# The first product of the down projection, its weight loads and its stores, in a one-core encoder layer in f32

## The chip, the cores and the metric

The kernel runs on one core of one Trainium2 chip. Times are microseconds of device time for one execution of the whole program; where several runs were made, the median is given. The core has a matrix engine (TensorE, PE), three engines for element-wise work (VectorE, DVE; ScalarE, ACT; GpSimd, POOL), a fifth engine that issues DMAs (SyncE, SP), and 16 DMA engines that move data between the chip's memory and the on-chip buffer. Each engine runs its own instructions in order; engines wait for one another by semaphores. ACT can issue DMAs too; those stand in its own order of instructions.

## The reference

One layer of an encoder: two attention branches merged by gates, and then a squared-ReLU MLP with a residual sum, and a final normalisation. The case touches only the MLP:

```python
h = _rmsnorm(x, g_mlp)
x = x + jnp.square(jax.nn.relu(h @ w_up)) @ w_down      # w_up 1024 x 4096, w_down 4096 x 1024
...
return _rmsnorm(x, g_final)
```

It is applied to 1024 sample tokens and to 256 prompt tokens with the same weights, 1280 rows in all, everything in float32.

## The kernel before

The attention half, up to about 950 us, is the same in both kernels. The MLP comes in two stages.

Each float32 product is made of three passes of TensorE over operands split in a rounded part (`hi`) and a remainder (`lo`): `lo` with `hi`, `hi` with `lo`, `hi` with `hi`. Splitting is done by ACT (the copy that rounds, `whi`, `dhi`, `uhi`) and then DVE (the subtraction that leaves the remainder, `wlo`, `dlo`, `ulo`). Both matrix products use a Strassen-like scheme: seven block products in place of eight, with sums and differences of blocks made beforehand. The names A11, A12, A22, S1 to S4 are those of the seven left operands.

*Up stage.* The function `up(j, ...)` runs for j = 0 to 15. Each pass makes the seven products for 256 columns of the hidden layer (PE tiles `x`, `y`, `z`, `pv`, `sc`), applies the squared ReLU (`relu2` on ACT, `relu2_sum` on DVE, into tiles `u`), makes four of the seven left operands of the down projection by sums on POOL, and stores all seven to a scratch array `scr_u` in memory with seven DMAs on SP. The weights of the next pass are split meanwhile. At fixed points of a pass a generator, `hooks`, is moved one step; in the last pass this is `Down.begin`, which prepares the start of the down projection.

*Down stage.* `Down.go` works through the list `JOBS` of 28 pairs (n, g): n is one of the seven products, g one of four groups of the hidden layer. Groups are taken in two pairs, and within a pair the order is n = 0 to 6, each for both groups. A job is 60 matmuls (PE tile `dn`): five tiles of rows, four blocks of the hidden layer, three passes. Its left operand is fetched from `scr_u` (`fetch`, three DMAs into `uraw`) two jobs ahead and split one job ahead (`left`: `uhi`, `ulo`, and for the prompt rows `up`). Its right operand is a block of `w_down` (`block`, two DMAs of 512 KB into `raw`) or a difference of blocks made by POOL (`combine`, tile `t`), split by `right` into `dhi` and `dlo`. `ORDER` gives the left operand of each n: S1, A11, S2, S3, S4, A22, A12. `TO` gives the blocks of the result, C11 to C22, to which product n is added; the sum is taken by DVE on tiles `v`, which begin as the residual, loaded from scratch `scr_x` by `residual` with five DMAs.

Around the change the order is written out by hand: instructions run on each engine in the order in which the code issues them. So a DMA on SP waits behind the DMAs ahead of it, and so does everything behind a DMA on ACT. A DMA takes one of eight completion semaphores in turn, and is held until the eighth DMA before it has landed. In `begin` the first two blocks of `w_down`, (0,0,0) and (0,0,1), are loaded by ACT's queue, and the first job is n = 0, whose right operand is a difference that POOL makes of these two.

Of the kernel before, what the change touches and what calls it, by code (L numbers as in the profile page):

```python
# [10 lines left out]
F32 = mybir.dt.float32  # L11
# [24 lines left out]
TH = T // 2  # L36

A11, A12, S2, S3, S1, A22, S4 = range(7)
# [59 lines left out]
def encoder_kernel(  # L98
# [5 lines left out]
    nc = tc.nc  # L104
# [13 lines left out]
    w_down4 = w_down[0].rearrange("(g k p) n -> p g k n", p=P, k=2)  # L118
# [37 lines left out]
    class Wide:  # L156
# [9 lines left out]
        def block(self, b):  # L166
            name, k, dt, make = self.spec
            n = BLOCKS[b][1]
            per = min(k, (self.most if b == 2 else 4096) // 4 // n)
            for i in range(k // per):  # L170
                self.t[b, i] = make(f"{name}_{b}_{i}", (P, per, n), dt)
# [461 lines left out]
    def entering():  # L633

        nonlocal unit0
        fetch()
        yield
        yield
        unit0 = load_unit(0), load_bias(0, wslot)
        yield  # L640
        prepare()
        yield
# [26 lines left out]
    with ExitStack() as pre:  # L669
        late = pre.enter_context(tc.tile_pool(name="values", bufs=1))  # L670
# [237 lines left out]
    if True:  # L908
# [4 lines left out]
        def stage(name, shape=(P, 512), dt=F32, n=1):  # L913
            pool = both if name in ("c", "z") else now[0]
            return pool.tile(list(shape), dt, name=name, tag=name, bufs=n)
# [739 lines left out]
    C11, C12, C21, C22 = range(4)  # L1655

    TO = ((C22, C12), (C11,), (C12,), (C21, C22), (C12,), (C21,), (C11,))
    JOBS = [(n, 2 * p + i) for p in range(NG // 2) for n in range(7) for i in range(2)]

    class Down:  # L1660
        def __init__(self):
# [3 lines left out]
        def make(self, name, shape=(P, 2, 512), dt=F32):  # L1665
            return self.late.tile(list(shape), dt, name=name, tag="l4", bufs=8)

        def block(self, g, k, h, make=wslot, queue=None):

            b = self.blocks[g, k, h] = [make("raw", (P, 2, 512)) for _ in range(2)]  # L1670
            for i in range(2):
                j = 4 * g + 2 * i
                (queue or nc.sync).dma_start(b[i], w_down4[:, j : j + 2, k, 512 * h : 512 * h + 512])

        def loads(self, n, g):
            if n == 1:
                self.block(g, 1, 1, slot)
            elif n == 4:
                self.block(g, 1, 0, slot)
            elif n == 5 and g < NG - 2:  # L1680
                self.block(g + 2, 0, 0)
                self.block(g + 2, 0, 1)

        def combine(self, n, g):

# [67 lines left out]

        def begin(self):

            self.block(0, 0, 0, wslot, nc.scalar)
            self.block(0, 0, 1, slot, nc.scalar)
            self.fetch(*JOBS[0])
            yield
            self.combine(*JOBS[0])  # L1760
            yield
            yield
            self.block(1, 0, 0)
            self.block(1, 0, 1)
            yield
            self.right(*JOBS[0], slot)
            self.combine(*JOBS[1])
            yield
            self.left(*JOBS[0], 0)
            self.left(*JOBS[0], 1)  # L1770
            yield
            self.fetch(*JOBS[1])
            yield
            self.left(*JOBS[0], 2)

        def ahead(self, s):

            n, g = JOBS[s]
            one, two = (JOBS[i] if i < len(JOBS) else None for i in (s + 1, s + 2))
            if two:  # L1780
                self.fetch(*two)
            self.loads(n, g)
            if s in (0, 2, 4):
                self.residual((C22, C11, C21)[s // 2])
            if s == 0:
                self.residual(C12)
            if one:
                self.right(*one, slot if s == 0 else self.make)
            if two:
                self.combine(*two)  # L1790
            yield
            for k in range(3):
                if one:
                    self.left(*one, k)
                yield
# [67 lines left out]
    with ExitStack() as pre:  # L1863
# [21 lines left out]
            yield x, y, c1  # L1885

        begun = {}

        def up(j, b, parts, hooks):

            def prompt_out(ps, dst):
                for i, d in enumerate(dst):
                    relu2(d[:, 512:], ps[:, P * i : P * i + P])

            u = [stage(f"u{i}", TH) for i in range(7)]
            u11, u12, u22, u21 = u[A11], u[A12], u[A22], u[S3]
            start = begin(parts)
            if j not in begun:  # L1900
                next(start)
            z = bank("sc", "z")
            nb = np_ = None
            steps_of(b, 2)
            next(hooks, None)
            x, y, c1 = begun[j] if j in begun else next(start)
            relu2_sum(u11[:, :512], y, c1)
            steps_of(b, 2)
            if j:
                pa = prompt(parts[0])  # L1910
            if j + 1 < FF // P // 2:
                np_ = []
                nb = right_up(j + 1, np_)
                next(nb)
            next(hooks, None)
            seven(x, S2, parts[1], 0, False, False)
            c2 = stage("c2", 512)
            nc.scalar.activation(c2, x, AF.Copy)
            if j:
                prompt_out(pa, (u11, u21))  # L1920
            steps_of(b, 2)
            next(hooks, None)
            seven(z, S3, parts[1], 1, last=False)
            c7 = stage("c7", 512)
            nc.scalar.activation(c7, z, AF.Copy)
            if not j:
                steps_of(nb, 2)
            next(hooks, None)
            seven(x, S1, parts[2], 0, False, False)
            relu2_sum(u22[:, :512], x, c7)  # L1930
            next(hooks, None)
            if nb and j:
                steps_of(nb, 3)
            seven(z, A22, parts[2], 1, False)
            relu2_sum(u21[:, :512], z, c2)
            next(hooks, None)
            if not j:
                *_, begun[1] = begin(np_)
            seven(x, S4, parts[3], 1, False)
            relu2(u12[:, :512], x)  # L1940
            next(hooks, None)
            if not j:
                steps_of(nb, 4)
                prompt_out(prompt(parts[0]), (u11, u21))
            prompt_out(prompt(parts[3], "sc"), (u12, u22))
            nc.gpsimd.tensor_tensor(u[S1], u21, u22, op=ALU.add)  # L1946
            nc.gpsimd.tensor_tensor(u[S2], u[S1], u11, op=ALU.subtract)
            nc.gpsimd.tensor_tensor(u[S3], u11, u21, op=ALU.subtract)
            nc.gpsimd.tensor_tensor(u[S4], u12, u[S2], op=ALU.subtract)
            for i in (A11, S1, A22, S2, S3, A12, S4):  # L1950
                nc.sync.dma_start(scr_u[j // 4][:, i, j % 4, :], u[i])
            next(hooks, None)
            return nb, np_

# [16 lines left out]
        down = Down()  # L1971
        last = FF // P // 2 - 1
        for j in range(last + 1):
            b = up(j, *b, entering() if not j else down.begin() if j == last else iter(()))

    down.go()

# [23 lines left out]
```

## Time and profile before

| what | before |
|---|---|
| median of three runs | 1692.16 us |
| the three runs | 1690.64, 1692.16, 1692.21 us |
| profiled execution, its own time | 1693.05 us |
| profiled execution, span | 1691.3 us |
| mean granted TensorE clock | 0.997 |
| PE busy | 1670.7 us (99%) |
| DVE, ACT, POOL busy | 950.1, 721.3, 514.9 us |

The span runs from the first to the last instruction of the profiled execution; its own time is 1.75 us more. In rows of the timeline the columns are the start, the time, the engine, the line, the operation with its output and inputs, and the shape; in square brackets stands how long the engine idled before it and what ended the idling. ACTq and SPq are the DMA issues on ACT and SP. In rows of waits the three numbers are the sum, the count and the longest. In rows of windows each engine has its busy time and, in parentheses, its number of instructions; behind them stand PEclk, the granted TensorE clock as a share of full speed, the mean share of the DMA engines in use, and the rate in GB/s.

### The profile page before, as it was taken

How to read it: one execution, taken by the hardware profiler on the slowest of the kernel's cores; microseconds unless marked ns; L12 is line 12 of the kernel's file. 1: busy time of each engine (PE TensorE's matmuls, PEld its weight loads, DVE VectorE, ACT ScalarE, POOL GpSimd, SP SyncE). 2: the span in 40 equal slices, each digit the busy share in tenths (PEclk: the TensorE clock that was granted, in tenths of full speed). 3: DMA queues.
4: the chain of work that ended last, by engine and by line, in shares of the span. 5: the costliest groups of instructions: out<-in, count | busy, mean ns of one | idle time of the engine just before them, and what ended most of it. 6: DMA issues, size and time to landing. Idle time of an engine off the chain costs nothing.

```text
span 1691.3 us, 24932 instructions
## 1 busy us (share of the span) xinstructions
PE 1670.7 (99%) x9268; PEld 1414.9 (84%) x9268; DVE 950.1 (56%) x1548; ACT 721.3 (43%) x1489; POOL 514.9 (30%) x404
## 2 busy tenths in 40 slices
PE   8999999999999999999999999999999999999998
PEld 7898888887788888888888888888887888888886
DVE  6733233455563565667378445455457767667575
ACT  6332323356562656654176333333334333333345
POOL 1312212212112472200100556455556322314150
PEclk9999999999999999999999999999999999999999
DMA  7416562567666893845121443343346744633333
GB/s 246 151 57 125 134 136 75 162 192 200 182 196 193 219 245 100 289 136 189 41 85 58 159 159 118 121 159 130 116 152 250 280 152 157 209 106 116 119 119 124
DMA packets 224408, 260.35 MB, mean 154 GB/s; under 512 B 29568, under 2 KB 154288, under 8 KB 224288
## 3 DMA queue, kind: packets, MB, share of 16 engines
q1 hardware_dynamic: 214976, 235.60, 43.9%
q0 software_dynamic: 7936, 20.54, 5.6%
q10 hardware_dynamic: 1376, 2.62, 0.4%
q8 instruction: 73, 1.20, 0.3%
q14 instruction: 47, 0.39, 0.1%
HBM read 173.03 MB, written 90.92 MB: 156 GB/s over the span
## 4 chain that ended last, share of the span: by engine, by line
PE 90%; DVE 4%; ACT 2%; DMA 2%; issue 1%; POOL 1%; SPq 0%; DVEq 0%; ACTq 0%; POOLq 0%
PE dn L347 20%; PE x L347 18%; PE mm L192 14%; PE z L347 9%; PE v L794 6%; PE mm L347 5%; PE y L347 5%; PE sc L347 2%; PE pv L347 2%; PE sc L537 1%; PE pv L1170 1%; PE pv L582 1%; PE pt L569 1%; PE pt L1155 1%; PE sc L1131 1%
## 5 line engine op out<-in xcount | busy, mean ns | idle before, releaser
L347 PE MATMUL dn<-dhi,ulo 128*128 128x512 f32 x448 | 175.7, 392 | 4.3 <-DVE ulo L186 4.3
L347 PE MATMUL dn<-dlo,uhi 128*128 128x512 f32 x448 | 175.2, 391 | 0.0
L347 PE MATMUL dn<-dhi,uhi 128*128 128x512 f32 x448 | 175.1, 391 | 0.0
L347 PE MATMUL x<-chi,wlo 128*128 128x512 f32 x424 | 167.3, 395 | 1.7 <-DVE wlo L314 1.6
L347 PE MATMUL x<-clo,whi 128*128 128x512 f32 x424 | 165.7, 391 | 0.1
L347 PE MATMUL x<-chi,whi 128*128 128x512 f32 x424 | 165.1, 389 | 0.0
L314 DVE TENSOR_TENSOR wlo<-ta,whi 128x1024 fp32r<-128x1024 f32 x30 | 55.7, 1857 | 179.1 <-ACT whi L312 179.1
L314 DVE TENSOR_TENSOR wlo<-raw,whi 128x1024 fp32r<-128x1024 f32 x60 | 92.5, 1541 | 96.7 <-ACT whi L312 96.7
L389 POOL TENSOR_TENSOR tb<-raw 128x512 f32<-128x512 f32 x25 | 32.7, 1308 | 364.4 <-DMA raw<-in_w_in_dram 147.8
L347 PEld LDWEIGHTS dn<-dhi,ulo 128*128 128x128 f32 x448 | 84.6, 189 | 23.2 <-DVE ulo L186 5.7
L186 DVE TENSOR_TENSOR ulo<-uraw,uhi 128x1024 fp32r<-128x1024 f32 x56 | 94.3, 1702 | 12.4 <-ACT uhi L185 12.4
L347 PEld LDWEIGHTS dn<-dhi,uhi 128*128 128x128 f32 x448 | 84.7, 189 | 17.8
L347 PEld LDWEIGHTS dn<-dlo,uhi 128*128 128x128 f32 x448 | 84.7, 189 | 17.4
L347 PEld LDWEIGHTS x<-chi,wlo 128*128 128x128 f32 x424 | 79.8, 188 | 18.1 <-DVE wlo L314 1.3
L347 PEld LDWEIGHTS x<-chi,whi 128*128 128x128 f32 x424 | 79.6, 188 | 17.0
L1699 POOL TENSOR_TENSOR t<-raw,t 128x1024 f32<-128x1024 f32 x16 | 47.7, 3001 | 147.0 <-DMA raw<-in_w_down_dram 147.0
L347 PEld LDWEIGHTS x<-clo,whi 128*128 128x128 f32 x424 | 79.8, 188 | 14.8 <-DVE clo L314 0.4
L1853 DVE TENSOR_TENSOR v<-v,dn 128x512 f32<-128x512 f32 x90 | 59.6, 681 | 40.4 <-PE dn L347 37.9
L1946 POOL TENSOR_TENSOR u<-u,u 128x640 f32<-128x640 f32 x16 | 26.1, 1630 | 160.0 <-ACT u L1871 160.0
L347 PE MATMUL dn<-dhi,up 128*128 128x512 f32 x224 | 73.5, 389 | 0.0
L347 PE MATMUL z<-chi,wlo 128*128 128x512 f32 x184 | 72.0, 391 | 0.0
L272 ACT ACTIVATE pt<-pt 128x512 f32<-128x512 f32 (+1 forms) x70 | 37.9, 543 | 79.5 <-PE pt L1155 45.0
(325 smaller groups left out, 4660.9 us busy)
## 6 DMA issues: line engine op xcount, KB each, us to landing
scr_u<-u SPq DMA_DIRECT2D x112, 320.0 KB, 2.6
uraw<-scr_u SPq DMA_DIRECT2D x56, 512.0 KB, 4.5
raw<-in_w_in_dram SPq DMA_DIRECT2D x33, 512.0 KB, 5.4
raw<-in_w_up_dram SPq DMA_DIRECT2D x32, 512.0 KB, 5.2
raw<-in_w_down_dram SPq DMA_DIRECT2D x28, 512.0 KB, 6.6
sg<-scr_g SPq DMA_DIRECT2D x32, 256.0 KB, 6.4
uraw<-scr_u SPq DMA_DIRECT2D x28, 256.0 KB, 4.7
v<-scr_v SPq DMA_DIRECT2D x96, 64.0 KB, 2.7
```

Source lines behind the costliest of these rows:

```text
L186: nc.vector.tensor_tensor(lo, src, hi.bitcast(F32), op=ALU.subtract)
L192: nc.tensor.matmul(ps, a, b, start=i == 0, stop=i == len(seq) - 1)
L272: nc.scalar.activation(out, in_, AF.Copy)
L314: nc.vector.tensor_tensor(lo, src, hi.bitcast(F32), op=ALU.subtract)
L347: nc.tensor.matmul(ps, a, b, start=first and i == 0, stop=last and i == len(seq) - 1, skip_group_check=True)
L389: (nc.vector if vector else nc.gpsimd).tensor_tensor(o, x, y, op=ALU.subtract)
L537: nc.tensor.matmul(at(k, h)[p0 : p0 + nq, :], qk[rows, p0 : p0 + nq], qk[rows, P + P * a : P + P * a + W], start=True, stop=True, skip_gro ...
L569: nc.tensor.transpose(ps[:, P * a : P * a + P], s[:, h, P * k : P * k + P], ident)
L794: nc.tensor.matmul(ps[:, :n], a, b, start=k == 0 and j == 0, stop=k == KC - 1 and j == 2)
L1699: nc.gpsimd.tensor_tensor(o, a, b, op=ALU.subtract)
L1853: nc.vector.tensor_tensor(v, v, ps, op=ALU.add)
L1946: nc.gpsimd.tensor_tensor(u[S1], u21, u22, op=ALU.add)
```

## The change

The first pair of groups now begins with n = 6, whose left operand is A12 and whose right operand is a plain block of `w_down`, (g,1,0), with no difference by POOL. The block for the first job is loaded in the pass before the last, into a buffer of the up stage; that for the second job in the last pass. All loads are issued by SP. The blocks (0,0,0) and (0,0,1) are loaded later in the last pass, (1,0,0) and (1,0,1) in the first job. The block (g,1,0) of the first pair is thus read twice, since the product n = 5 still needs it. The first blocks of the next pair are loaded with n = 4 in place of n = 5. The residual blocks are loaded one per job, C11 first. The seven stores of a pass are issued in the next pass behind its first products and its first hook. In the last pass the split of the right operand (`right`) stands at the third hook, ahead of the product S3, and the split of the left operand (`left`) follows the sum for `u22`.

```diff
-    JOBS = [(n, 2 * p + i) for p in range(NG // 2) for n in range(7) for i in range(2)]
+    JOBS = [(n, 2 * p + i) for p in range(NG // 2) for n in (range(7) if p else (6, *range(6))) for i in range(2)]
...
-        def block(self, g, k, h, make=wslot, queue=None):
+        def block(self, g, k, h, make=wslot):
...
-                (queue or nc.sync).dma_start(b[i], w_down4[:, j : j + 2, k, 512 * h : 512 * h + 512])
+                nc.sync.dma_start(b[i], w_down4[:, j : j + 2, k, 512 * h : 512 * h + 512])
 
         def loads(self, n, g):
-            if n == 1:
+            if n == 6 and g == 0:
+                self.block(1, 0, 0)
+                self.block(1, 0, 1)
+            elif n == 1:
                 self.block(g, 1, 1, slot)
             elif n == 4:
                 self.block(g, 1, 0, slot)
-            elif n == 5 and g < NG - 2:
-                self.block(g + 2, 0, 0)
-                self.block(g + 2, 0, 1)
+                if g < NG - 2:
+                    self.block(g + 2, 0, 0)
+                    self.block(g + 2, 0, 1)
...
         def begin(self):
 
-            self.block(0, 0, 0, wslot, nc.scalar)
-            self.block(0, 0, 1, slot, nc.scalar)
             self.fetch(*JOBS[0])
             yield
-            self.combine(*JOBS[0])
-            yield
-            yield
-            self.block(1, 0, 0)
-            self.block(1, 0, 1)
+            self.block(1, 1, 0)
             yield
             self.right(*JOBS[0], slot)
-            self.combine(*JOBS[1])
+            yield
+            self.fetch(*JOBS[1])
             yield
             self.left(*JOBS[0], 0)
             self.left(*JOBS[0], 1)
-            yield
-            self.fetch(*JOBS[1])
+            self.block(0, 0, 0)
+            self.block(0, 0, 1)
             yield
             self.left(*JOBS[0], 2)
...
-            if s in (0, 2, 4):
-                self.residual((C22, C11, C21)[s // 2])
-            if s == 0:
-                self.residual(C12)
+            if s < 4:
+                self.residual((C11, C22, C12, C21)[s])
...
+        stores_u = []
+
+        def store_u():
+            while stores_u:
+                nc.sync.dma_start(*stores_u.pop(0))
...
             next(hooks, None)
+            store_u()
+            u = [stage(f"u{i}", TH) for i in range(7)]
+            u11, u12, u22, u21 = u[A11], u[A12], u[A22], u[S3]
...
-            for i in (A11, S1, A22, S2, S3, A12, S4):
-                nc.sync.dma_start(scr_u[j // 4][:, i, j % 4, :], u[i])
+            stores_u.extend((scr_u[j // 4][:, i, j % 4, :], u[i]) for i in (A11, S1, A22, S2, S3, A12, S4))
...
+            if j == last - 1:
+                down.block(0, 1, 0, lambda name, shape: late.tile(list(shape), F32, name=name, tag="block", bufs=2))
             b = up(j, *b, entering() if not j else down.begin() if j == last else iter(()))
+        store_u()
```

The change moves instructions on the engines; three places show how. First SP, at the end of the last pass but one and in the last pass of the up stage. `scr_u_106` and `scr_u_107` are the groups 0 and 1 of the scratch array, `scr_u_109` group 3, which the last passes fill. Before:

```order
L1951 DMA scr_u_109<-u_12195 128x640
L1719 DMA uraw<-scr_u_106 128x2x512 x2
L1721 DMA uraw<-scr_u_106 128x4x128
L1673 DMA raw<-in_w_down_dram 128x2x512 x4
L1719 DMA uraw<-scr_u_107 128x2x512 x2
L1721 DMA uraw<-scr_u_107 128x4x128
L1951 DMA scr_u_109<-u_12392 128x640
```

And after the change:

```order
L377 DMA raw<-in_w_up_dram 128x8x128 x2
L1722 DMA uraw<-scr_u_106 128x2x512 x2
L1724 DMA uraw<-scr_u_106 128x4x128
L1888 DMA scr_u_109<-u_12214 128x640
L1888 DMA scr_u_109<-u_12218 128x640
L1888 DMA scr_u_109<-u_12219 128x640
L1888 DMA scr_u_109<-u_12216 128x640
L1888 DMA scr_u_109<-u_12217 128x640
L1888 DMA scr_u_109<-u_12215 128x640
L1888 DMA scr_u_109<-u_12220 128x640
L1673 DMA raw<-in_w_down_dram 128x2x512 x2
L1722 DMA uraw<-scr_u_107 128x2x512 x2
```

The seven stores of the last pass but one stood ahead of the first job's fetch and now stand behind it; two weight loads, those of the second job, stand behind the stores.

Second ACT, from the middle of the last pass to the start of the down projection (`c` are copies of a PE result, `u` the squared ReLU, `whi` the split of up weights, `dhi` and `uhi` that of a down job's right and left operand). Before:

```order
L1882 ACTIVATE c_12413<-x 128x512
L312 ACTIVATE whi<-ta 128x1024
L1673 DMA raw<-in_w_down_dram 128x2x512 x4
L312 ACTIVATE whi<-tb 128x1024
L1918 ACTIVATE c_12493<-x 128x512
L1870 ACTIVATE u_12392<-pv 128x128
L1871 ACTIVATE u_12392<-u_12392 128x128
L1870 ACTIVATE u_12395<-pv 128x128
L1871 ACTIVATE u_12395<-u_12395 128x128
L312 ACTIVATE whi<-raw 128x1024
L1925 ACTIVATE c_12515<-z 128x512
L185 ACTIVATE dhi<-t_12477 128x1024
```

And after:

```order
L312 ACTIVATE whi<-ta 128x1024
L312 ACTIVATE whi<-tb 128x1024
L1920 ACTIVATE c_12489<-x 128x512
L1866 ACTIVATE u_12423<-pv 128x128
L1867 ACTIVATE u_12423<-u_12423 128x128
L1866 ACTIVATE u_12426<-pv 128x128
L1867 ACTIVATE u_12426<-u_12426 128x128
L312 ACTIVATE whi<-raw 128x1024
L185 ACTIVATE dhi<-raw 128x1024 x2
L1927 ACTIVATE c_12519<-z 128x512
L185 ACTIVATE uhi<-uraw 128x1024 x2
L185 ACTIVATE up<-uraw 128x512
```

The four DMA issues between `whi<-ta` and `whi<-tb` are gone; both `dhi` now come from raw weights and stand ahead of the copy of `z`, and the two `uhi` directly behind it.

Third SP, as the down projection begins (`v` are the tiles of the result, `scr_x_96` to `scr_x_105` the rows of the residual). Before:

```order
L1951 DMA scr_u_109<-u_12398 128x640
L1719 DMA uraw<-scr_u_106 128x2x512 x2
L1721 DMA uraw<-scr_u_106 128x4x128
L1752 DMA v<-scr_x_100 128x512
L1752 DMA v<-scr_x_101 128x512
```

And after:

```order
L1888 DMA scr_u_109<-u_12429 128x640
L1722 DMA uraw<-scr_u_106 128x2x512 x2
L1724 DMA uraw<-scr_u_106 128x4x128
L1673 DMA raw<-in_w_down_dram 128x2x512 x4
L1755 DMA v<-scr_x_96 128x512
L1755 DMA v<-scr_x_97 128x512
L1755 DMA v<-scr_x_98 128x512
L1755 DMA v<-scr_x_99 128x512
L1755 DMA v<-scr_x_104 128x512
L1722 DMA uraw<-scr_u_107 128x2x512 x2
```

The last store and the third job's fetch stand as they did; four weight loads now stand between that fetch and the residual, of which C11 is the first block and five tiles are loaded in a job instead of ten.

More of the change, by code (lines that the diff above doesn't have):

```diff
@@ L1895, in prompt_out @@
                     relu2(d[:, 512:], ps[:, P * i : P * i + P])
-            u = [stage(f"u{i}", TH) for i in range(7)]
-            u11, u12, u22, u21 = u[A11], u[A12], u[A22], u[S3]
             start = begin(parts)
```

## The prediction

> **What bounds the kernel now.** I read first the busy time of each engine, then the waits of TensorE in the MLP half (950 us to the end).
>
> ```profile
> span 1691.3 us, 24932 instructions
> PE 1670.7 (99%) x9268; PEld 1414.9 (84%) x9268; DVE 950.1 (56%) x1548; ACT 721.3 (43%) x1489; POOL 514.9 (30%) x404
> PE dn L347 <- DVE ulo L186: 4.3, 3, 3.2
> ```
>
> TensorE (PE) is the bound. The change adds and removes no matmul, so only PE's waits and its pace can move the end. In the MLP half it waited three times, 4.3 us in all (longest 3.2), each time for a left-operand remainder `ulo`. The timeline of PE shows where:
>
> ```profile
> 1287.72 0.39 PE L347 MATMUL z<-chi,wlo 128*128 128x512 f32 x1
> ...
> 1296.09 0.28 PE L347 MATMUL sc<-phi,whi 128*128 128x256 f32 x1
> 1299.56 0.80 PE L347 MATMUL dn<-dhi,ulo 128*128 128x512 f32 x1 [3.19 <-DVE ulo L186]
> 1302.87 0.80 PE L347 MATMUL dn<-dhi,ulo 128*128 128x512 f32 x1 [0.38 <-DVE ulo L186]
> 1305.68 0.40 PE L347 MATMUL dn<-dlo,uhi 128*128 128x512 f32 x1
> ...
> 1316.34 0.39 PE L347 MATMUL dn<-dhi,ulo 128*128 128x512 f32 x1
> 1616.45 0.50 PE L347 MATMUL dn<-dhi,ulo 128*128 128x512 f32 x1 [0.75 <-DVE ulo L186]
> ```
>
> Two waits stand where the down projection begins: its first job starts at 1299.56, its second at 1316.34. The third, at 1616.45, is in a job that the change leaves in its place; I leave it as it is. The windows view (PE with its matmul count, then the other engines, PEclk, DMA share, GB/s) shows that the wait also cost pace:
>
> ```profile
> 1299.50:1305.60 6.10, 5.66 (x13) 4.02 (x14) 6.10 (x4) 2.13 (x3) 6.02 (x3) 0.53 0.11 40
> 1305.60:1310.00 4.40, 4.40 (x22) 3.60 (x21) 4.40 (x3) 0.00 (x0) 4.40 (x3) 1.00 0.58 220
> 1315.00:1340.00 25.00, 25.00 (x112) 20.71 (x111) 20.04 (x20) 8.20 (x9) 6.21 (x2) 1.00 1.05 375
> 1616.40:1622.00 5.60, 5.55 (x24) 4.62 (x25) 4.60 (x5) 1.20 (x4) 0.00 (x0) 1.00 0.80 249
> ```
>
> After the 3.19 us wait the granted clock was 0.53 for some 6 us; after the 0.75 us wait it stayed at 1.00.
>
> Why was `ulo` late? ScalarE (ACT; ACTq are its DMA issues), last pass of the up stage:
>
> ```profile
> 1232.80 0.60 ACT L1918 ACTIVATE c<-x 128x512 f32<-128x512 f32 x1 [5.85 <-PE x L347]
> 1257.64 0.60 ACT L1918 ACTIVATE c<-x 128x512 f32<-128x512 f32 x1 [5.85 <-PE x L347]
> 1259.16 1.04 ACT L312 ACTIVATE whi<-raw 128x1024 fp32r<-128x1024 f32 x1
> ...
> 1274.14 0.60 ACT L1882 ACTIVATE c<-x 128x512 f32<-128x512 f32 x1 [1.62 <-PE x L347]
> ...
> 1274.71 7.21 ACTq L1673 DMA_DIRECT2D raw<-in_w_down_dram  x3
> 1281.96 1.06 ACT L312 ACTIVATE whi<-tb 128x1024 fp32r<-128x1024 f32 x1 [6.28 <-DMA scr_u<-u]
> ...
> 1292.11 1.06 ACT L185 ACTIVATE dhi<-t 128x1024 fp32r<-128x1024 f32 x1 [2.28 <-POOL t L1699]
> ```
>
> One pass over j takes 24.84 us (1232.80 to 1257.64). In the last pass ACT stood 6.28 us in its own DMA issues, behind stores, and later for POOL's difference `t` (here 2.28). VectorE (DVE) follows ACT:
>
> ```profile
> 1260.24 1.23 DVE L314 TENSOR_TENSOR wlo<-raw,whi 128x1024 fp32r<-128x1024 f32 x1 [3.52 <-ACT whi L312]
> 1278.34 0.68 DVE L1874 TENSOR_TENSOR u<-y,c 128x512 f32<-128x512 f32 x1
> ...
> 1283.06 1.23 DVE L314 TENSOR_TENSOR wlo<-tb,whi 128x1024 fp32r<-128x1024 f32 x1 [2.67 <-ACT whi L312]
> ...
> 1290.45 2.18 DVE L1875 SCALAR_TENSOR_TENSOR u<-u 128x512 f32<-128x512 f32 x1
> 1292.55 2.35 DVE L186 TENSOR_TENSOR dlo<-t,dhi 128x1024 fp32r<-128x1024 f32 x2
> ...
> 1296.14 6.68 DVE L186 TENSOR_TENSOR ulo<-uraw,uhi 128x1024 fp32r<-128x1024 f32 x2
> 1304.71 5.09 DVE L186 TENSOR_TENSOR dlo<-t,dhi 128x1024 fp32r<-128x1024 f32 x2
> 1323.03 1.22 DVE L186 TENSOR_TENSOR ulo<-uraw,uhi 128x1024 fp32r<-128x1024 f32 x1
> ```
>
> The same `ulo` takes 3.34 us while POOL works (6.68 for two) and 1.22 alone.
>
> **The change part by part.** *The start of down (a gain).* The last up matmul starts at 1296.09, and its neighbours follow one another at 0.12, so the first down matmul could start at 1296.21. It starts at 1299.56: 3.35 lost. A job has 60 matmuls; the 47 steps from 1305.68 to 1316.34 take 0.2268 each, so a job takes 13.61. The first took 16.78: 3.17 lost to the half clock and the small wait. Together 6.52.
>
> Does the new order reach 1296.21? The first job now takes raw weights (no `t` from POOL), loaded a whole pass earlier, and ACT issues no DMA, so ACT keeps the cadence of the pass before: `whi<-raw` at 1259.16+24.84 = 1284.0, two `dhi` at 1.07 to 1287.2, the copy c (0.60) to 1287.8, two `uhi` to 1290. (PE's product `z` at 1287.72 needs that copy done: 0.1 late, within the rounding.) On DVE `wlo` ends at 1286.4, two `dlo` (2.35) at 1288.8, the sum and its square (0.68, at most 2.18) at 1291.7, two `ulo` (2.44, POOL being idle) at 1294.1. That is 2.1 early, so all 6.52 comes back. By the worst row, `ulo` at 3.34 each, it would be 1298.4, 2.2 late: the low end of the gain is 6.52−2.2 = 4.3 if the clock then holds.
>
> The first job's two loads move into the pass before, the second job's two to the start of the last pass: each 1.4 at 375 GB/s, with more than 10 us before `dhi` wants them. Zero.
>
> What the new order moves on the queues (timeline rows of SP and POOL, and rows of DMA issues, which end with KB each and median us to landing):
>
> ```profile
> 1258.78 21.42 SPq L1951 DMA_DIRECT2D scr_u<-u  x7
> 1311.66 0.93 SPq L1719 DMA_DIRECT2D uraw<-scr_u  x2
> 1312.69 0.47 SPq L1721 DMA_DIRECT2D uraw<-scr_u  x1
> scr_u<-u SPq DMA_DIRECT2D x112, 320.0 KB, 2.6
> uraw<-scr_u SPq DMA_DIRECT2D x1, 256.0 KB, 9.4
> 1301.69 2.54 POOL L1946 TENSOR_TENSOR u<-u,u 128x640 f32<-128x640 f32 x1
> ...
> 1308.68 2.54 POOL L1949 TENSOR_TENSOR u<-u,u 128x640 f32<-128x640 f32 x1
> 1286.33 2.40 POOL L1699 TENSOR_TENSOR t<-raw 128x1024 f32<-128x1024 f32 x1 [6.49 <-PE x L347]
> ```
>
> *The stores of the pass before the last.* They now queue on SP behind the fetch of the first job's left operand, which waits for a buffer until PE has gone through its first product: 1274.1 at the latest, when ACT copies that product. The slowest fetch around here landed in 9.4, so the operand is there by 1284.9 (1.4 of issue, 9.4); ACT needs it at 1287.8: no cost. The first store starts by 1275.5 instead of 1258.78. It must have landed before DVE overwrites its `u`, at 1278.34. With the 2.6 of the 112 stores it has, at 1278.1; with 9.4 DVE starts 6.6 late. What PE next needs of DVE is `wlo<-tb`, which so far was done at 1284.3 after 2.67 us of idling; that idling takes up the first 2.7. I take 0, by the 2.6; the other end is 3.9.
>
> *Second job, weights.* Two raw `dlo` and two `ulo` follow from about 1298.5. At 2.55 each (5.09 for two, beside POOL) they end at 1308.7, at 3.34 at 1311.9; the job starts at 1296.21+13.61 = 1309.8 and needs its second half by 1311.2. Zero, at most 0.7.
>
> *Third job (a loss).* It starts at 1309.8+13.61 = 1323.4. Its left operand comes out of DVE's in-order stream, which now has the first residual additions ahead of it: the residual block is wanted one pair earlier. POOL's four sums took 9.53 (1301.69 to 1311.22) beside DVE; they begin now at 1297.4, when the last `u` is done, and end at 1306.9. SP sends the last store and at 1307.2 the fetch. The rows for what follows (DMA issues, then one of DVE's timeline):
>
> ```profile
> uraw<-scr_u SPq DMA_DIRECT2D x1, 256.0 KB, 5.4
> raw<-in_w_down_dram SPq DMA_DIRECT2D x28, 512.0 KB, 6.6
> 1322.42 0.69 DVE L1853 TENSOR_TENSOR v<-v,dn 128x512 f32<-128x512 f32 x1 [2.48 <-DMA v<-scr_x]
> ```
>
> The fetch lands 6.4 after its first issue (1.03 until its third part is issued at 1312.69, then 5.4): 1313.6. Behind it go four weight loads of 512 KB and the first residual tile of 256 KB, 2.36 MB; at the 375 GB/s of the row above 6.3, so the first `v` lands at 1319.9. DVE: `v` add 0.69 to 1320.6; `ulo` beside POOL's `t` (2 x 2.40, whose weights have just landed) 3.34 to 1323.9; a second `v` add; the second `ulo` 1.22 to 1325.8. The third job needs its second half six matmuls after its start, at 1324.8. So PE waits 1.0. Before, DVE had the same wait at 1322.42 and PE's cover held. With `v` 1 us earlier the loss is 0; at 280 GB/s `v` comes 2.1 later and the loss is 3.1. A short wait keeps the full clock, as at 1616.45.
>
> *Four more weight loads* (block (g,1,0) is read a second time, 2.1 MB), and the loads moved from n=5 to n=4: they land in 6.6 at the median, and are issued a job (13.61) or more ahead of their use. Zero; 1.4 each (512 KB at 375) if that cover is gone. The Trainium skill's page "DMA: Bandwidth & Descriptors", section "Issuing engines are not separate DMA queues", says that issues from several engines share the 16 DMA engines and that spreading them saves only issue time; by it, giving ACT's four loads to SP would change the time by nothing but the 6.28 us in ACT's row, and this trace does show that as an in-order wait, not as transfer time.
>
> Sum: −6.52 + 1.0 = −5.5. The profiled execution took 1693.05 (span 1691.3 and 1.75 around it): 1687.5. The median of the three runs, 1692.16, lies 0.89 under it: **1686.7**.
>
> **The rivals.** *The clock loss is not there in each execution.* For: a wait of 0.75 left the clock at 1.00, one of 3.19 halved it, so the threshold is somewhere between, and runs without a profile may miss it. Then the gain is 3.35−1.0 = 2.35: 1689.8. The Trainium skill ("TensorE: Matmul & The Clock Gate", "What's actually happening") puts the idle time needed at about 3.4 us in a free-running window: by it a 3.35 gap stands on the edge.
>
> *A new wait takes the place.* If the third job waits for more than about 2, the clock may halve again (3.2 as above): −6.5+2.2+3.2 = −1.1 at 2.2, 1691.1; with 3.1 it is about 1692. For: all loads are on one queue and `v` is last in it; against: 375 GB/s in 1315 to 1340 with just such traffic.
>
> *The change does nothing at the start*, because the operand is late for another reason (its fetch, or the stores holding DVE at 1278): 1692.2.
>
> *Slower.* One mechanism: the queue at the third job. 3.7 MB of fetches, loads and residual lie ahead of what DVE needs; at 220 GB/s rather than 375 `v` lands 7 us later, PE waits 8 and loses 3.2 more: −6.5+11.2, 1696.9. It decides for slower once `v` lands 6 later than 1319.9. Only the 220 GB/s of 1305.60 to 1310.00 speaks for it, and there too little was asked for.
>
> **How the numbers follow.** The main case 0.72 (1685.2 to 1688.4: third-job wait 0 to 2.2, the runs' own spread); clock 0.08; new wait 0.08 (1689 to 1693); nothing 0.06; slower 0.06. Within 0.2% (3.4 us, about what measurement can tell) ends at 1688.8. That gives faster 0.76, same 0.18, slower 0.06. The range 1684.8 to 1691.0 holds the main case, the clock case and part of the new wait, 0.82.
>
> **What would show it.** In the changed kernel's profile: no PE wait ahead of the first down matmul and PEclk 1.00 there; no ACT DMA issue in that pass; a PE wait near 1 for `ulo` 27 us after the first down matmul, with DVE waiting for `v` ahead of it; the 0.75 wait still there. Wrong if `dhi` or `uhi` starts after 1290, if DVE waits for a store at its sum of y, or if the third job's wait is over 2.

## The result

| | before | changed |
|---|---|---|
| median of 7 runs each | 1692.16 us | 1687.79 us |
| lowest to highest | 1690.56 to 1695.35 us | 1686.26 to 1688.91 us |
| profiled execution, its own time | 1693.05 us | 1688.11 us |
| profiled execution, span | 1691.3 us | 1686.3 us |

The ratio of the runs is 0.9971, with a 95% interval of 0.9961 to 0.9981: faster by 4.9 us (3.2 to 6.6); the medians lie 4.4 apart. The forecast was 1686.7, in a range of 1684.8 to 1691.0. When the changed kernel was measured again beside one of the experiments below, the ratio was 0.9964 (0.9951 to 0.9976).

The page of the changed kernel and TensorE's (PE's) waits from 950 us to the end:

```profile
PE 1670.2 (99%) x9268; PEld 1414.6 (84%) x9268; DVE 948.2 (56%) x1548; ACT 720.7 (43%) x1489; POOL 510.7 (30%) x404
PE dn L347 <- DVE ulo L186: 0.7, 1, 0.7
```

Of three waits for `ulo`, 4.3 us in all, one of 0.7 us is left: the one in the job that the change did not move. The timeline of PE, from the last matmuls of the up stage on:

```profile
1296.73 0.28 PE L347 MATMUL sc<-phi,whi 128*128 128x256 f32 x1
1296.86 0.40 PE L347 MATMUL dn<-dhi,ulo 128*128 128x512 f32 x1
...
1323.86 0.39 PE L347 MATMUL dn<-dhi,up 128*128 128x512 f32 x1
1324.26 0.47 PE L347 MATMUL dn<-dhi,ulo 128*128 128x512 f32 x1
...
1325.49 0.40 PE L347 MATMUL dn<-dhi,uhi 128*128 128x512 f32 x1
1325.95 0.50 PE L347 MATMUL dn<-dhi,ulo 128*128 128x512 f32 x1
1326.29 0.40 PE L347 MATMUL dn<-dlo,uhi 128*128 128x512 f32 x1
...
1611.26 0.50 PE L347 MATMUL dn<-dhi,ulo 128*128 128x512 f32 x1 [0.73 <-DVE ulo L186]
```

The down projection now follows the up stage at 0.13 us. The next irregular steps come two jobs later: 0.40 into 1324.26 and 0.46 into 1325.95, where a step is 0.23; the step behind each is longer too (0.34 into 1326.29). They carry no bracket, being shorter than a listed wait, but they are the third job starting late. The windows view says that the clock stayed whole at both places (columns as before; PEclk is the third from the right):

```profile
1296.86:1303.00 6.14, 6.14 (x29) 5.07 (x28) 3.83 (x2) 5.38 (x9) 4.66 (x3) 1.00 0.26 100
1324.26:1330.00 5.74, 5.68 (x24) 4.34 (x25) 5.74 (x8) 2.76 (x3) 0.00 (x0) 1.00 1.07 372
```

ScalarE (ACT) and VectorE (DVE) in the last pass, and the third job's operand on DVE:

```profile
1258.46 0.60 ACT L1920 ACTIVATE c<-x 128x512 f32<-128x512 f32 x1 [5.84 <-PE x L347]
...
1275.46 1.05 ACT L312 ACTIVATE whi<-ta 128x1024 fp32r<-128x1024 f32 x1
1276.40 1.05 ACT L312 ACTIVATE whi<-tb 128x1024 fp32r<-128x1024 f32 x1
...
1285.77 1.99 ACT L185 ACTIVATE dhi<-raw 128x1024 fp32r<-128x1024 f32 x2
...
1288.15 2.00 ACT L185 ACTIVATE uhi<-uraw 128x1024 fp32r<-128x1024 f32 x2
```

```profile
1290.64 2.35 DVE L186 TENSOR_TENSOR ulo<-uraw,uhi 128x1024 fp32r<-128x1024 f32 x2
...
1320.30 0.69 DVE L1849 TENSOR_TENSOR v<-v,dn 128x512 f32<-128x512 f32 x1 [4.44 <-DMA v<-scr_x]
1320.91 3.25 DVE L186 TENSOR_TENSOR ulo<-uraw,uhi 128x1024 fp32r<-128x1024 f32 x1
1324.09 0.67 DVE L1849 TENSOR_TENSOR v<-v,dn 128x512 f32<-128x512 f32 x1
1324.68 1.21 DVE L186 TENSOR_TENSOR ulo<-uraw,uhi 128x1024 fp32r<-128x1024 f32 x1
```

ACT issues no DMA in this pass and goes straight from `whi<-ta` to `whi<-tb`. Both `ulo` of the first job are done at 1292.99, 3.9 us before PE needs them. The third job's two `ulo` end at 1324.16 and 1325.89, and PE's two late starts follow each by 0.1 or less.

One thing has to be kept apart. ACT's copy `c` with 5.84 or 5.85 us of idling ahead stands in each kernel in the last pass but one, before anything differs that PE waits for: at 1257.64 before, at 1258.46 now. The 0.82 us between them already stand at ACT's first copy `c` of the up stage (899.61 and 900.43); from there to this row both kernels take 358.03, although the change also moves the stores of the earlier passes. So the part of the program that the change does not touch took 0.82 us more in this profiled execution. Over all the profiles of this case that row stands between 1255.16 and 1258.72. I therefore count from it, in two pieces: to the first down matmul, and from there to the start of the last one (a job at full pace is 13.60, and 28 of them, less the last step, 380.6):

| | copy to first down matmul | first to last down matmul | sum | against before |
|---|---|---|---|---|
| before | 41.92 | 384.80 | 426.72 | |
| changed | 38.40 | 382.30 | 420.70 | −6.02 |

This measure stops at the start of the last matmul. From there to the end of the span it is 6.90 us before and 7.17 now, and 7.17 to 7.22 in every kernel below that has the new order of products, against 6.91 in the one that has the old. What makes this 0.3 us is not shown. Counted from the copy to the end of the span, the change brings 5.75.

### The profile page after: what moved, and what is told of

The parts are those of the page before. It is cut to its first block, busy times and chain, and to the rows that moved or that the text cites. A ratio compares the mean times of both kernels' runs of the same rounds, so it can differ in the third digit from the quotient of the medians.

```text
span 1686.3 us, 24914 instructions
## 1 busy us (share of the span) xinstructions
PE 1670.2 (99%) x9268; PEld 1414.6 (84%) x9268; DVE 948.2 (56%) x1548; ACT 720.7 (43%) x1489; POOL 510.7 (30%) x404
## 5 line engine op out<-in xcount | busy, mean ns | idle before, releaser
L186 DVE TENSOR_TENSOR ulo<-uraw,uhi 128x1024 fp32r<-128x1024 f32 x56 | 90.0, 1628 | 10.4 <-ACT uhi L185 10.4
L186 DVE TENSOR_TENSOR dlo<-raw,dhi 128x1024 fp32r<-128x1024 f32 x32 | 47.5, 1506 | 45.7 <-ACT dhi L185 44.8
```

The source lines that it names most:

```text
L186: nc.vector.tensor_tensor(lo, src, hi.bitcast(F32), op=ALU.subtract)
```

## The experiments

Two theories of why the first job was late before. *P*: its right operand was a difference that POOL made of blocks only just loaded, with DVE slowed beside POOL. *Q*: ACT stood 6.28 us in its own DMA issues. The change cures both at once. All kernels of this part, in the same measure:

| | copy to first down matmul | first to last | sum | against before | median, runs |
|---|---|---|---|---|---|
| loads on SP alone | 40.06 | 383.70 | 423.76 | −2.96 | 1689.58, 10 |
| product order alone | 39.30 | 382.30 | 421.60 | −5.12 | 1686.88, 7 |
| changed, stores at the end of a pass | 38.40 | 382.16 | 420.56 | −6.16 | 1686.93, 10 |
| changed, residual first | 38.39 | 381.63 | 420.02 | −6.70 | 1686.25, 6 |
| changed, three repeats | 39.57 | 381.79 | 421.36 | −5.36 | 1686.80, 1 |
| changed, four repeats | 40.83 | 383.37 | 424.20 | −2.52 | 1688.82, 1 |
| changed, five repeats | 43.30 | 383.89 | 427.19 | +0.47 | 1692.57, 1 |
| changed, more loads | 38.39 | 382.52 | 420.91 | −5.81 | 1685.04, 1 |
| changed, both waits removed | 38.39 | 380.60 | 418.99 | −7.73 | 1685.61, 5 |
| changed again | 38.39 | 382.29 | 420.68 | −6.04 | 1686.25, 5 |

The changed kernel's two profiles agree within 0.02 us in this measure, while whole times of one kernel spread over 1 to 7 us. So the trace decides below, and the medians only confirm.

**The loads alone on SP**

```diff
-            self.block(0, 0, 0, wslot, nc.scalar)
-            self.block(0, 0, 1, slot, nc.scalar)
+            self.block(0, 0, 0)
+            self.block(0, 0, 1, slot)
```

> The kernel before, with ACT's four weight loads issued by SP in the same place of the code; the product order stays (S1 first, its right operand a difference by POOL). Theory P (POOL's difference t of two blocks that are only just loaded holds the first job): ACT runs on without its 6.28 us hold, but t still waits for the weights, now issued by SP behind the seven stores, and dhi for t; PE waits 2.5 to 4.5 us for the first down matmul, its first job takes about 16.8 us, and the time is that of before within 0.15%. Theory Q (ACT's hold in its own DMA issues makes the operand late): the wait at the first down matmul is gone, the first job takes 13.6 us, and the time is 5 to 6.5 us below before.

The ratio to before was 0.9984 (0.9975 to 0.9994). PE's timeline, and windows that hold its two waits:

```profile
1296.05 0.50 PE L347 MATMUL dn<-dhi,ulo 128*128 128x512 f32 x1 [1.51 <-DVE ulo L186]
...
1299.37 0.50 PE L347 MATMUL dn<-dhi,ulo 128*128 128x512 f32 x1 [1.67 <-DVE ulo L186]
```

```profile
1291.76:1295.17 3.41, 2.78 (x24) 2.57 (x22) 3.34 (x5) 3.38 (x5) 0.20 (x1) 1.00 1.05 387
1295.17:1298.59 3.42, 1.65 (x6) 1.05 (x6) 3.42 (x2) 1.93 (x7) 3.42 (x2) 1.00 1.06 374
1298.59:1302.00 3.41, 2.63 (x11) 2.17 (x12) 3.41 (x2) 1.13 (x2) 3.41 (x2) 1.00 0.29 101
```

ACT in the same kernel, and one split of up weights on DVE, in the kernel before and in this one:

```profile
1288.41 1.06 ACT L185 ACTIVATE dhi<-t 128x1024 fp32r<-128x1024 f32 x1 [4.26 <-POOL t L1699]
1291.21 1.06 ACT L185 ACTIVATE dhi<-t 128x1024 fp32r<-128x1024 f32 x1 [1.74 <-POOL t L1699]
```

```profile
1286.36 3.45 DVE L314 TENSOR_TENSOR wlo<-raw,whi 128x1024 fp32r<-128x1024 f32 x1 [2.08 <-ACT whi L312]
```

```profile
1283.42 1.23 DVE L314 TENSOR_TENSOR wlo<-raw,whi 128x1024 fp32r<-128x1024 f32 x1 [3.52 <-ACT whi L312]
```

Neither theory's numbers came out. PE still waits, as P says, and ACT still stands for POOL's `t`; but the start comes 1.86 us sooner, and the first job takes 15.70 instead of 16.78. ACT's hold did cost something. It pushed the split of up weights on DVE under POOL's `t`, where it took 3.45 us; without the hold it is done in 1.23, before POOL begins at 1285.97. And one long wait became two short ones, each of which leaves the clock whole. Three of the six microseconds could be had by this edit of two lines.

**The product order alone**

```diff
...
+            self.block(0, 0, 0, wslot, nc.scalar)
+            self.block(0, 0, 1, slot, nc.scalar)
             self.fetch(*JOBS[0])
...
             self.left(*JOBS[0], 1)
-            self.block(0, 0, 0)
-            self.block(0, 0, 1)
...
+            store_u()
             next(hooks, None)
             return nb, np_
```

> The changed kernel with the queues of before: the blocks (0,0,0) and (0,0,1) are loaded by ACT at the first hook and the stores are issued at the end of a pass; A12 stays first, its weights loaded a pass ahead. ACT should stand some 6 us in its DMA issues again. Theory P: no wait at the first down matmul all the same, or under 1 us, first job 13.6 us; since dhi stands ahead of the copy of z, PE may wait about 1.3 us in the up stage for that copy; the time is 4 to 6 us below before. Theory Q: PE waits about 3 us for the first down matmul, the first job takes 16.8 us, the time is that of before.

This kernel keeps everything of the change but the queue and place of the two blocks that ACT loads and the place of the stores: it also has the first job's loads a pass ahead, the new places of the splits and the new order of the residual. The ratio to before was 0.9967 (0.9956 to 0.9978). ACT stood in its DMA issues again, and PE's only other wait beside the old one is at the product `z`:

```profile
1273.05 6.93 ACTq L1673 DMA_DIRECT2D raw<-in_w_down_dram  x3
1280.02 1.06 ACT L312 ACTIVATE whi<-tb 128x1024 fp32r<-128x1024 f32 x1 [6.00 <-DMA raw<-in_w_down_dram]
...
1286.21 0.57 ACT L1927 ACTIVATE c<-z 128x512 f32<-128x512 f32 x1
1287.70 1.06 ACT L185 ACTIVATE uhi<-uraw 128x1024 fp32r<-128x1024 f32 x1 [0.91 <-DMA uraw<-scr_u]
```

```profile
1286.84 0.50 PE L347 MATMUL z<-chi,wlo 128*128 128x512 f32 x1 [0.61 <-ACT c L1927]
```

P's forecast, with the new wait at half its guessed size. No wait stands ahead of the first down matmul. The plain product, loaded ahead, with what goes with it brings 5.1 us of the 6.0; the queues add 0.9 to it, though by themselves they bring 3.0. The two causes overlap: either cure alone saves the clock.

**The stores at the end of a pass again**

```diff
+            store_u()
             next(hooks, None)
             return nb, np_
```

> The changed kernel with the seven stores issued at the end of a pass as before; all else as changed. The first job's fetch then goes out behind the last store, near 1281 in place of 1273, and lands 1286 to 1290; ACT wants it at 1288. Theory P: with 2 us of room on DVE, PE waits 0 to 0.5 us at the first down matmul and the time is within 1 us of the changed kernel. If the later stores are what brings the gain, PE waits 1.5 us or more there, the time is 2 to 5 us above the changed kernel.

```profile
1257.41 21.45 SPq L1888 DMA_DIRECT2D scr_u<-u  x7
1278.90 0.97 SPq L1722 DMA_DIRECT2D uraw<-scr_u  x2
```

The same places in the changed kernel:

```profile
1257.49 16.24 SPq L1722 DMA_DIRECT2D uraw<-scr_u  x2
1273.84 0.41 SPq L1724 DMA_DIRECT2D uraw<-scr_u  x1
1274.35 6.68 SPq L1888 DMA_DIRECT2D scr_u<-u  x7
```

Counted from the copy, the fetch began to go out at 22.6 us here (1278.90, the copy standing at 1256.27), and had gone out at 15.8 in the changed kernel (1274.25), when its buffers had come free; ACT waited for it in neither. The start is the same to 0.01 us and the sum 0.14 us lower. Issuing the stores later brings nothing in the traced execution.

**The residual ahead of the weights**

```diff
-            self.loads(n, g)
             if s < 4:
                 self.residual((C11, C22, C12, C21)[s])
+            self.loads(n, g)
```

> The changed kernel with the residual's five tiles issued ahead of the weight loads in each job. If the third job's 0.7 us is lost because the residual's first tile lands behind four weight loads (2.1 MB), that tile lands about 5.5 us earlier, the second and third job take 13.6 us each, and the fourth, whose difference by POOL now starts 3.5 us later, still has over 8 us of room: 0.7 us less from the first to the last down matmul than in the changed kernel. The rival, that DVE's pace beside POOL makes the third job late, leaves the loss at 0.5 or more, or moves it to the fourth job. The total is within noise of the changed kernel in both cases; the profile decides.

DVE at the third job:

```profile
1314.53 0.68 DVE L1849 TENSOR_TENSOR v<-v,dn 128x512 f32<-128x512 f32 x1
1315.13 1.22 DVE L186 TENSOR_TENSOR ulo<-uraw,uhi 128x1024 fp32r<-128x1024 f32 x1
1316.27 0.68 DVE L1849 TENSOR_TENSOR v<-v,dn 128x512 f32<-128x512 f32 x1
1316.86 1.22 DVE L186 TENSOR_TENSOR ulo<-uraw,uhi 128x1024 fp32r<-128x1024 f32 x1
```

The first sum runs 4.5 us sooner than in the changed kernel (18.9 us after the first down matmul instead of 23.4) and without waiting for `v`; both `ulo` take 1.22 with POOL still idle. Jobs two, three and four take 13.60 each: the 0.67 us that the third job had lost are back, and the fourth job, whose `t` now starts later, does not wait. The forecast's cause is shown.

**Holding the first operand back**

DVE makes the first `ulo` again n times, which changes no value:

```diff
+            uhi, ulo = self.lefts[JOBS[0]][0]
+            for _ in range(n):
+                nc.vector.tensor_tensor(ulo, self.raw[JOBS[0]][0], uhi.bitcast(F32), op=ALU.subtract)
             self.left(*JOBS[0], 2)
```

> The changed kernel in which DVE makes the first job's first ulo three times more, behind the sum u from z, so that PE has to wait for it. Each repeat takes about 1.2 us while POOL is idle, and DVE was done 2.6 us ahead of need, so PE waits about 0.9 us for the first down matmul. Theory H (a long enough wait halves the clock, the bound lying between the 1.8 us that left it whole and the 3.2 us that halved it): the first job takes 13.6 us behind its start. Rival (any wait at this place halves the clock): 16.5 us or more.

> The same with four repeats: the fourth runs beside POOL's sums, so PE waits 2.0 to 2.5 us. Theory H leaves it open on which side of the bound that lies: 13.6 us for the first job behind its start if the clock stays whole, 16 to 17 us if it halves for some 6 us. The rival: 16.5 us or more.

> The same with five repeats: PE waits 3.3 to 5.5 us, over the 3.2 us of the kernel before. Theory H: the clock halves, and the first job takes 16 to 17 us behind its start although no weight or left operand is late any more but the one held back. Rival (the slow first job of the kernel before came from its late operands, not from the clock): 13.6 to 14 us.

The first down matmul with three repeats, and the window behind it:

```profile
1296.01 0.50 PE L347 MATMUL dn<-dhi,ulo 128*128 128x512 f32 x1 [1.01 <-DVE ulo L1774]
```

```profile
1296.01:1302.00 5.99, 5.99 (x26) 4.96 (x27) 5.41 (x4) 4.46 (x6) 5.69 (x3) 1.00 0.40 153
```

With four repeats:

```profile
1296.48 0.50 PE L347 MATMUL dn<-dhi,ulo 128*128 128x512 f32 x1 [2.27 <-DVE ulo L1774]
```

```profile
1294.46:1297.87 3.41, 1.39 (x6) 1.17 (x7) 3.38 (x3) 3.35 (x7) 2.41 (x1) 1.00 0.00 0
1297.87:1301.28 3.41, 3.41 (x10) 2.64 (x9) 3.41 (x3) 1.81 (x3) 3.35 (x2) 0.50 0.67 261
1301.28:1304.70 3.42, 3.42 (x16) 2.79 (x16) 3.42 (x2) 0.00 (x0) 3.42 (x2) 1.00 0.52 205
```

With five:

```profile
1299.70 0.80 PE L347 MATMUL dn<-dhi,ulo 128*128 128x512 f32 x1 [4.75 <-DVE ulo L1774]
```

```profile
1294.07:1297.49 3.42, 0.88 (x8) 0.68 (x6) 3.32 (x4) 2.44 (x6) 1.30 (x1) 1.00 0.02 9
1297.49:1304.31 6.82, 4.61 (x11) 3.64 (x12) 6.82 (x4) 2.93 (x4) 6.74 (x4) 0.50 0.43 169
1304.31:1307.73 3.42, 3.42 (x17) 2.81 (x16) 3.42 (x2) 0.00 (x0) 3.42 (x2) 1.00 0.65 246
```

The slow first job comes from the clock and not from late operands: with all other operands early, a wait of 4.75 us makes the first job 15.88 us, one of 2.27 makes it 15.37, and one of 1.01 makes it 13.75. Together with the two waits of the first experiment, the clock stayed whole up to 1.67 us and halved from 2.27. These are single executions; where exactly the bound lies stays open. At 2.27 PE ran 1.4 us at full pace first (1296.48 to 1297.87) and was slowed only then, so the answer comes late. The half clock lasted 3.41 us there, and with five repeats 6.83 (1297.49 to 1304.31), the first 2.2 of them still in the wait.

The length of the wait alone does not decide, though. In these profiles the granted clock changes only at the edges of cells of 3.41 us: the half clock lasts one cell with four repeats and two with five and in the kernel before (1298.41 to 1305.24), and in all three it is 382.29 us from the end of that stretch to the next change, at the end of the program, which is 112 cells. Counted back from that last change, the cells can also be laid where the clock stayed whole; the windows shown for the first experiment and for four and five repeats are such cells (1297.49 to 1304.31 is two). In the cell ahead of each halving PE idled, by its length less PE's busy time, 2.02 us (four repeats), 2.54 (five) and, in the kernel before, 2.04:

```profile
1295.00:1298.41 3.41, 1.37 (x12) 1.17 (x10) 3.38 (x3) 2.76 (x8) 2.36 (x2) 1.00 1.06 375
```

The first experiment's two waits add up to 3.18, as much as the one wait of 3.19 before, but they fall into three cells (0.63, 1.77 and 0.78), and no halving follows. Over whole profiles, the most that PE idled in a cell at full clock without a halving behind it is 1.87, at the end of the kernel with both waits removed (1676.55 to 1679.97). So what these profiles show is a bound on the idling within one cell, between 1.87 and 2.02 us. At half clock less is enough to stay there: in the kernel before, the cell from 1298.41 had 1.15 us of idling, and the next was still at half clock. Where the cells fall differs from one execution to the next: the first edge behind the first down matmul comes 0.86 us later in the changed kernel and 1.65 later in the one with more loads.

The three repeats show another thing: PE waited 1.01 us (the start came 1.18 later) and lost only 0.66 in the sum, since the third job, starting later, found its operand ready (13.60).

**More loads**

```diff
             elif n == 4:
                 self.block(g, 1, 0, slot)
+                self.block(g, 1, 0, slot)
```

> The changed kernel in which the block (g,1,0) is read once more with n = 4 in each of the four groups, into slots that nothing reads: eight more loads, 4.2 MB. If the second reading of that block costs nothing because its loads land well ahead of use, the time from the first to the last down matmul stays at 382.3 us within 0.3. If the loads are on the path, it grows by up to 1.4 us each, 11 us; a partial price of 1 to 5 us would mean that the slots, held for loads nobody needs, delay the fetches behind them.

From the first to the last down matmul 382.52 us, 0.22 more, and those 0.2 lie in the third job (14.02 and 14.06 us for the second and third), ahead of any of the added loads. So 4.2 MB more cost nothing that shows. That the 2.1 MB of the change's own second reading cost nothing either is argued from this; no run leaves them out.

**Both remaining waits removed**

```diff
-            elif n == 4:
+            elif n == 3 and g >= NG - 2:
+                self.block(g, 1, 0)
+            elif n == 4 and g < NG - 2:
                 self.block(g, 1, 0, slot)
...
-            self.loads(n, g)
             if s < 4:
                 self.residual((C11, C22, C12, C21)[s])
+            self.loads(n, g)
...
-                self.combine(*two)
+                early = [(5, g) for g in range(NG - 2, NG)]
+                if two not in early:
+                    self.combine(*two)
+                if two[0] == 4 and (5, two[1]) in early:
+                    self.combine(5, two[1])
```

> The changed kernel with the residual ahead of the weight loads and, in the last pair of groups, the block (g,1,0) loaded with n = 3 and the difference t for n = 5 made by POOL two jobs sooner. If the 0.73 us wait at the twenty-fourth job is due to DVE's dlo and ulo running beside POOL's t (4.9 and 4.6 us for two in place of 2.4), that wait goes too, and the first to the last down matmul takes 380.6 us, 28 jobs of 13.6, against 382.3 in the changed kernel: some 1.7 us (0.1%) below it in the total. Rival: DVE is late there for its sums v or ACT's squares ahead of dhi; then a wait of 0.4 us or more stays, or t earlier makes another job wait.

> The changed kernel once more, on the same chip as the run above: from the first to the last down matmul 382.3 us, and the time 1.0 to 2.4 us above the run above if what its trace loses is what the clock outside sees.

DVE ahead of the twenty-fourth job, in the changed kernel:

```profile
1602.99 4.87 DVE L186 TENSOR_TENSOR dlo<-raw,dhi 128x1024 fp32r<-128x1024 f32 x2 [1.74 <-ACT dhi L185]
1607.78 4.55 DVE L186 TENSOR_TENSOR ulo<-uraw,uhi 128x1024 fp32r<-128x1024 f32 x2
```

and with POOL's `t` made two jobs sooner:

```profile
1603.05 2.67 DVE L186 TENSOR_TENSOR dlo<-raw,dhi 128x1024 fp32r<-128x1024 f32 x2 [1.74 <-ACT dhi L185]
1605.64 2.35 DVE L186 TENSOR_TENSOR ulo<-uraw,uhi 128x1024 fp32r<-128x1024 f32 x2
```

Every job takes 13.60 us (the first 13.63), and the down projection 380.60: in the trace TensorE waits for nothing in it any more. That is 1.69 us below the changed kernel run beside it. The medians, 1685.61 and 1686.25, point the same way, but their ratios to before, 0.9959 (0.9946 to 0.9973) and 0.9964 (0.9951 to 0.9976), overlap: a gain of 0.1% is shown by the trace only.

## Why the prediction was right

- *The start, 3.35 forecast.* It came back whole: the first down matmul follows the last up matmul by 0.13 instead of 3.47 us. The up stage's last pass was 0.18 shorter besides, which the forecast did not have. The margin on DVE was forecast at 2.1 us and measured at 3.9, mostly because the square took 0.69 and not the 2.18 of a row beside POOL.
- *The first job, 3.17 forecast.* 16.78 became 13.63: 3.15. That the clock and not the operands made it slow was argued from two rows, and the repeats show it.
- *The stores, 0 within 0 to 3.9.* 0. The sum of y began at 1279.35, 0.2 us later than the pass before (1254.34 and 24.84 make 1279.18), and PE waited for nothing behind it.
- *The second job, 0 within 0 to 0.7.* 0.
- *The third job, 1.0 forecast within 0 and 3.1.* 0.67 to 0.68: 13.78 and 14.10 for the second and third job instead of twice 13.60. The mechanism, its place and its order on DVE were as forecast. Only the size was off: `v` landed 23.4 us after the first down matmul instead of 23.7, DVE's steps were some 0.1 shorter each, and of the loss some 0.4 are the two late starts of PE, most of the rest the longer steps behind them.
- *The extra loads, 0.* 0.
- *The job at 1616.45, left alone.* 14.51 before, 14.49 now.
- *Sum.* −6.02 in the measure above, −5.5 forecast. The untouched part of the program took 0.82 more in that profiled execution and the end of the program 0.27 more, which made the span 4.9 shorter. The end was in the sum at nothing, without a word on it; that with it the trace gives −5.75, still nearer to −5.5, is luck.

Of the rivals, the one that the clock loss is not there in each execution is in part true. The mean granted clock is on record for each run of the changed kernel and for each run made beside an experiment. In the traces it is 0.997 where the clock halves for two cells, 0.998 for one, and 0.999 or more where it stays whole. Of the 24 runs of the kernel before beside the first experiments, 11 have 0.997, 4 have 0.998 and 9 have 0.999 or 1.000 (the median is 1692.84 us for the 11 and 1691.22 for the 9); of the nine beside the last two experiments, 5, 1 and 3. All runs of the changed kernel have 0.999 or 1.000, and so have the ten with the loads on SP alone. The main case took the loss as certain, because the one traced execution had it; the rival took it as absent throughout, which would have left 3.52 − 0.68, 2.8 us, and the intervals of the runs (3.2 to 6.6, and 4.1 to 8.3 in the second measurement) lie above that. That the mixture is why the runs gained 4.4 to 4.9 us and the traced execution 5.75 fits, but is not shown. That of a new wait was real as a mechanism, but short of the length that halves the clock: up to the first `v` (1309.43 to 1320.30) the transfers ran at 370 GB/s, near the 375 assumed.

One step was told too simply. The prediction named two causes of the late `ulo`, ACT's hold and POOL's `t`, and gave neither a price of its own. They are not additive: alone the one is worth 3.0 and the other 5.1 us, together 6.0.

## What to carry to other kernels

At the seam between two stages, begin with the piece of work that needs the fewest steps from memory to the matrix engine, and load it a stage ahead. Price a wait of the matrix engine with the clock that it may cost: here the second wait of the first experiment, 1.67 us, cost 1.94 and the clock stayed whole, while that of 2.27 cost 4.2 (2.44 at the start, 1.75 in the job behind it). So splitting a long wait or shortening it a little can bring more than its own length. Whether a wait costs the clock can differ from one execution to the next, so one profile does not settle it. Read gains of a fraction of a per cent from a row that both kernels share just ahead of the change, since the rest of the program can move by more than the gain.

## What the runs showed that was not expected

- The clock halves already after a wait of 2.27 us, and not at once but 1.4 us after the work has resumed (1.00, then 0.50 for 3.41 us, then 1.00). The Trainium skill's page "TensorE: Matmul & The Clock Gate", section "What's actually happening", has the half clock follow at least one idle window of about 3.4 us; here cells in which PE idled only 2.02 to 2.54 us were enough, so the measurement decides. That the windows run freely, as the same section has it, agrees with these traces: the cells are 3.41 us long and do not begin with the kernel's own work.
- The kernel before loses the clock at this place in most of its runs, but not in all (0.997 or 0.998 in 21 of the 33 beside the experiments with several runs).
- Two DMA-issue lines on ACT, taken by themselves, cost 3 us, although DMA issues are not counted as busy time and ACT was busy for 43% of the span. The Trainium skill's page "DMA: Bandwidth & Descriptors", section "Issuing engines are not separate DMA queues", calls what issuing costs an engine usually small beside the DMA; here the issues stood in line behind stores, and the engine's other work behind them.
- A wait of 1.01 us put in at the first down matmul cost 0.66 in the end, as it paid for the wait of the third job.
- The part of the program ahead of the change differs by up to 3.6 us from one profiled execution to the next (the copy at 1255.16 to 1258.72); the runs of the changed kernel differ by 2.7 and 3.4 in its two series.
